# The first MLP product of a hybrid decoder layer, by Strassen's seven block products

## The chip, the cores and the metric

One core of a Trainium2 chip runs the whole layer as one program. The metric is the device time in microseconds; of the kernel before there are three runs, 825.94, 825.32 and 824.52 us, with the median 825.32.

## The reference, cut to what matters

One layer for 512 tokens of 1024 features, in float32. A token mixer of three gated branches (pooling, short convolution, dilated attention) is followed by an MLP with a hidden width of 4096. The change concerns the last two lines:

```python
h = rms_norm(x, norm_mix);  z = h @ w_in            # 1024 -> 7424 columns
merged = g0*(y_pool @ w_pool_up) + g1*(y_conv @ w_conv_out) + g2*(y_attn @ w_attn_up)
x = x + merged @ w_o
h2 = rms_norm(x, norm_mlp)
x = x + square(relu(h2 @ w_ff1)) @ w_ff2            # 1024 -> 4096 -> 1024
```

## The kernel before

Everything is held transposed: features lie on the 128 partitions, the 512 tokens along the free dimension, so x is eight tiles of 128x512. Weights are a stream of units of 128x1024 float32 in the order of use, loaded by SP's queue into three raw buffers (`unit`, L107). `split` (L115) writes each unit as the sum of two float32r parts: ScalarE copies the high part (L118), VectorE subtracts it from the raw unit for the low part (L119). Activations are split in the same way. `mm3` (L122) then makes a float32 product of three float32r matmuls: high by high, high by low, low by high (L125 to L127).

The program is traced in Python and a scheduler lays out each engine's instruction queue: what is ready by its own reckoning goes first, the earlier traced first among these; each queue then runs in that order on the chip, waiting for semaphores.

After the mixer, W_o goes to eight PSUM banks. `x2_evac` (L555) adds a bank to the residual (`res`, L556) and splits it times the norm's gain to `h2` (L164, L167). The first MLP product takes two units at a time, each 128 hidden features by all eight chunks of h2 (L581 to L587): 32 units, 24 matmuls of 128x512 each. 1/rms of x comes later, from squares on ScalarE (L196), their sum over the eight tiles on GpSimd (L200) and over partitions by a matmul with ones (L204); as it is positive, it is multiplied in after the product (L576), with the relu, and ScalarE squares (L577). The second product accumulates eight banks over 32 units (L602 to L610), and the residual is added and stored (L613, L614). All tiles of the mixer keep their memory to the end; the 32 hidden tiles take over those of `br` and `mg`.

Of the kernel before, what the change touches and what calls it, by code (L numbers as in the profile page):

```python
# [11 lines left out]
F32 = mybir.dt.float32  # L12
# [6 lines left out]
P = 128  # L19
# [16 lines left out]
NFF = 32  # L36
AHEAD = 1  # units of weights split ahead of their use
WARM = 9  # products of zeros that wake the tensor engine's clock until the first data is there
# [11 lines left out]
def z_order():  # L50
    """The 128-column chunks of w_in, as (kind, index, first column), in the order of use."""
    def qkv(p):
        return [(n, (g, p), off + (2 * g + p) * P)
                for g in range(3) for n, off in (("q", OFF_Q), ("k", OFF_K), ("v", OFF_V))]

    def conv(i):
        return [(n, i, off + i * P) for n, off in (("cc", OFF_C), ("cx", OFF_X), ("cb", OFF_B))]

    pool = [("pool", g, OFF_POOL + g * P) for g in range(4)]
    z = qkv(0) + conv(0) + conv(1) + qkv(1) + pool + conv(2) + conv(3)  # L60
    gates = [[("gate", (n, m), OFF_G + n * D + m * P) for n in range(3)] for m in range(KC)]
    return z, gates
# [3 lines left out]
def hybrid_layer(ctx: ExitStack, tc: tile.TileContext, xT, wst, pmix, vecs, consts, outT):  # L66
# [4 lines left out]
    wpool = ctx.enter_context(tc.tile_pool(name="wpool", bufs=3))  # L71
    apool = ctx.enter_context(tc.tile_pool(name="apool", bufs=1))
    ps = ctx.enter_context(tc.tile_pool(name="ps", bufs=8, space=PSUM))
# [10 lines left out]
    def tmp(dt=F32):  # L84
        return apool.tile([P, S], dt, tag="tmp", bufs=13, name=nm("tmp"))

# [11 lines left out]

# [1 line left out]
    ahead = deque()  # L100
    rp = None
    n_loaded = [0]

    def raw_unit():
        return wpool.tile([P, 1024], F32, tag="raw", bufs=3, name=nm("raw"))

    def unit():  # L107
        while len(ahead) <= AHEAD and n_loaded[0] < wst.shape[0]:
            raw = raw_unit()
            nc.sync.dma_start(raw, wst[n_loaded[0]])  # L110
            ahead.append(split(raw, rp if n_loaded[0] in LONG else wpool))
            n_loaded[0] += 1
        return ahead.popleft()
# [17 lines left out]

# [1 line left out]
    warm = cpool.tile([P, S], BF16, name="warm")  # L133
    nc.vector.memset(warm, 0.0)
# [16 lines left out]
    n_loaded[0] = KC // 2  # L151
    cst = cpool.tile([P, NCONST], F32, name="cst")
    nc.sync.dma_start(cst, consts)
# [4 lines left out]
    nc.vector.memset(epst, EPS)  # L158
    bd = cpool.tile([P, P], F32R, name="bd")

# [9 lines left out]
    def rsqrt_start(total, n):  # L170
        """1 / sqrt(total / n + EPS): by ln and exp, and what then takes one Newton step in float32."""
        v = tmp()
        nc.scalar.activation(v, total, AF.Identity, scale=1.0 / n, bias=epst)
        y = tmp()
        nc.scalar.activation(y, v, AF.Ln)
        nc.scalar.activation(y, y, AF.Exp, scale=-0.5)
        t = tmp()
        nc.scalar.activation(t, y, AF.Square)

        def newton(out):  # L180
            nc.vector.scalar_tensor_tensor(t, t, -0.5, v, op0=OP.mult, op1=OP.mult)
            out = t if out is None else out
            nc.vector.scalar_tensor_tensor(out, t, 1.5, y, op0=OP.add, op1=OP.mult)
            return out

        return newton

    class Rstd:
        """1 / rms over the features, from their squares as they come in."""

# [11 lines left out]
        def end(self, name):  # L202
            b = bank()
            nc.tensor.matmul(b, ones, self.acc, start=True, stop=True)  # L204
            r = cpool.tile([P, S], F32, name=name)
# [27 lines left out]

    # Work that hangs on a chunk of z goes on in steps, one after each later chunk.
    side = deque()
# [9 lines left out]

# [1 line left out]
    at = ExitStack()  # L247
    atp = at.enter_context(tc.tile_pool(name="atp", bufs=1))
# [34 lines left out]
    def v_evac(kind, idx, b):  # L283
# [20 lines left out]
    def attention(p):  # L304
        """Heads 2p and 2p + 1 of each group; keys on partitions. The groups' mixture is one softmax
        over the keys of all three: one maximum, one denominator."""
        q = [qkv["q", (g, p)] for g in range(3)]
# [65 lines left out]
        for h in range(2):  # L373
# [34 lines left out]

# [1 line left out]
    cu = [atp.tile([P, S + 2], F32, name=f"cu{i}") for i in range(2)]  # L410
# [29 lines left out]
    def load_mix():  # L440
        raw = raw_unit()
        nc.sync.dma_start(raw[:, :4 * P], pmix)
        hi = cpool.tile([P, 4 * P], F32R, name="mixh")
        lo = cpool.tile([P, 4 * P], F32R, name="mixl")
        nc.scalar.activation(hi, raw[:, :4 * P], AF.Copy)
# [51 lines left out]

# [1 line left out]
    res = []  # L499
# [12 lines left out]
    for m in range(KC):  # L512
# [10 lines left out]
        if m == 0:  # L523
            while side:
                pump()
            at.close()
            rp = ctx.enter_context(tc.tile_pool(name="rp", bufs=1))
            for k in range(KC):
                t = rp.tile([P, S], F32, name=f"res{k}")
# [17 lines left out]
        if m >= 1:  # L547
# [3 lines left out]
            wo_mm(0, m - 1, wo_banks[:4])  # L551
    h2 = [None] * KC
    rs2 = Rstd()

    def x2_evac(m):  # L555
        nc.vector.tensor_tensor(res[m], res[m], wo_banks[m], OP.add)  # L556
        h2[m] = split_gain(res[m], vec[:, V_NF + m:V_NF + m + 1], True)

    for i in range(4, 8):
# [3 lines left out]
    wo_mm(0, KC - 1, wo_banks[:4])  # L563
    for m in range(4):
        x2_evac(m)
    wo_mm(1, KC - 1, wo_banks[4:])
    for m in range(4, 8):
        x2_evac(m)

# [1 line left out]
    f = []  # L571

    def ff1_evac(pair):
        for b in pair:
            t = br(F32) if len(f) < 20 else mg(F32)
            nc.vector.scalar_tensor_tensor(t, b, 0.0, rstd2, op0=OP.max, op1=OP.mult)  # L576
            nc.scalar.activation(t, t, AF.Square)  # L577
            f.append(t)

    done = []  # L580
    for j in range(0, NFF, 2):  # L581
        pair = [bank(), bank()]
        w2 = [unit(), unit()]
        for ks in ([range(4)] + [range(k, k + 1) for k in range(4, KC)] if j == 0 else [range(KC)]):
            for b, w in zip(pair, w2):
                for k in ks:
                    mm3(b, w, cols(k), h2[k], k == 0, k == KC - 1)  # L587
        done.append(pair)
        if j == 0:
            for t in res:  # L590
                rs2.add(t)
        if j >= 2:
            if j == 2:
                rstd2 = rs2.end("rstd2")
            for pair in done:
                ff1_evac(pair)
            done = []

# [9 lines left out]
    for m in range(KC):  # L608
# [3 lines left out]
        for t, eng in zip(parts, (nc.sync, nc.scalar)):  # L612
            nc.vector.tensor_tensor(res[m][:, t], res[m][:, t], outs[m][:, t], OP.add)  # L613
            eng.dma_start(outT[:, m, t], res[m][:, t])  # L614


def _chunk(w, c):
    """Columns c..c+127 of w: [1024, n] as a unit [128, 8 * 128]."""
    return w[:, c:c + P].reshape(KC, P, P).transpose(1, 0, 2).reshape(P, KC * P)


def _stream(w_in, w_pool_up, w_conv_out, w_attn_up, w_o, w_ff1, w_ff2):
# [23 lines left out]
    for kk in range(4):  # L646
        units.append(wo(1, kk))
    for j in range(NFF):
        units.append(_chunk(w_ff1, j * P))
    for k in range(NFF):  # L650
# [54 lines left out]
```

## Time and profile before

| | |
|---|---|
| median of three runs | 825.32 us |
| profiled execution, first to last instruction | 822.6 us |
| TensorE matmul / weight load busy | 807.4 / 662.4 us |
| VectorE, ScalarE, GpSimd busy | 424.2, 297.7, 63.2 us |
| first MLP product | 464.95 to 644.42 us |
| second MLP product | from 644.42 us, last matmul about 818.7 us |

Of the profiled execution the page gives the span alone; the median of the timed runs stands 2.7 us above it. In the profile PE is TensorE's matmul, PEld its weight load, DVE VectorE, ACT ScalarE, POOL GpSimd, SP the engine that issues most DMAs. A busy time is the sum of an engine's instruction records; matmul records overlap one another, so the spacing of their starts, not their length, tells their rate.

### The profile page before, as it was taken

What the parts mean: (1) busy time and instruction counts of PE and PEld (TensorE: products, weight loads), DVE (VectorE), ACT (ScalarE), POOL (GpSimd) and SP (SyncE); (2) the same over time, 40 slices, a digit from 0 to 9 for tenths busy, and PEclk for the clock granted to TensorE, in tenths of its full rate; (3) what the DMA queues carried; (4) which work ended last, traced back from release to release, by engine and by line L of the source; (5) the groups of instructions that cost most, each with busy time, mean ns of one, the idle gap of its engine ahead of it and who ended that gap; (6) DMA issues with size and microseconds to landing.
All of it is one profiled execution on the core that took longest, in us unless ns stands there. A gap on an engine that the chain in (4) does not pass through costs nothing. (4 is left out here: it accounts for less than half of the span.)

```text
span 822.6 us, 9086 instructions
## 1 busy us (share of the span) xinstructions
PE 807.4 (98%) x3649; PEld 662.4 (81%) x3649; DVE 424.2 (52%) x530; ACT 297.7 (36%) x398; POOL 63.2 (8%) x50
## 2 busy tenths in 40 slices
PE   7999998999999999999999999999999999999998
PEld 4888787887888888888888778888888888888886
DVE  7659686786885434554343756333333333333323
ACT  5466255742363223322232527233223332233210
POOL 6020012124200000000000320000000000000000
PEclk9999999999999999999999999999999999999999
DMA  6422221221254222222222222222222232222312
GB/s 226 154 78 82 97 77 52 90 103 52 77 166 142 100 79 103 103 102 89 91 102 77 73 106 103 96 85 102 103 103 88 91 103 102 99 83 101 102 52 102
DMA packets 24810, 80.99 MB, mean 98 GB/s; under 512 B 2880, under 2 KB 3136, under 8 KB 24768
## 3 DMA queue, kind: packets, MB, share of 16 engines
q1 hardware_dynamic: 23472, 78.19, 27.3%
q10 hardware_dynamic: 1296, 2.23, 0.9%
q8 instruction: 28, 0.46, 0.2%
q14 instruction: 14, 0.11, 0.0%
HBM read 78.31 MB, written 2.10 MB: 98 GB/s over the span
## 5 line engine op out<-in xcount | busy, mean ns | idle before, releaser
L118 ACT ACTIVATE wh<-raw 128x1024 fp32r<-128x1024 f32 x136 | 144.0, 1060 | 406.6 <-issue 212.4
L127 PE MATMUL bank<-xs,wl 128*128 128x512 f32 x720 | 280.7, 390 | 3.6 <-DVE wl L220 2.4
L125 PE MATMUL bank<-xs,wh 128*128 128x512 f32 x720 | 282.0, 393 | 1.8 <-ACT tmp L196 1.8
L126 PE MATMUL bank<-xs,wh 128*128 128x512 f32 x720 | 280.9, 390 | 2.3 <-DVE xs L167 2.2
L119 DVE TENSOR_TENSOR wl<-raw,wh 128x1024 fp32r<-128x1024 f32 x136 | 170.1, 1252 | 68.5 <-ACT wh L118 64.0
L127 PEld LDWEIGHTS bank<-xs,wl 128*128 128x128 f32 x720 | 135.2, 188 | 33.2 <-DVE wl L220 3.4
L126 PEld LDWEIGHTS bank<-xs,wh 128*128 128x128 f32 x720 | 135.2, 188 | 32.9 <-DVE xs L167 4.8
L125 PEld LDWEIGHTS bank<-xs,wh 128*128 128x128 f32 x720 | 135.1, 188 | 31.8 <-ACT tmp L196 2.7
L126 PE MATMUL bank<-tmp,wh 128*128 128x512 f32 x256 | 99.6, 389 | 0.0
L125 PE MATMUL bank<-tmp,wh 128*128 128x512 f32 x256 | 99.6, 389 | 0.0
L127 PE MATMUL bank<-tmp,wl 128*128 128x512 f32 x256 | 99.6, 390 | 0.0
L127 PEld LDWEIGHTS bank<-tmp,wl 128*128 128x128 f32 x256 | 48.0, 188 | 10.2 <-DVE wl L119 0.3
L126 PEld LDWEIGHTS bank<-tmp,wh 128*128 128x128 f32 x256 | 48.1, 188 | 10.0
L125 PEld LDWEIGHTS bank<-tmp,wh 128*128 128x128 f32 x256 | 48.1, 188 | 9.9
L518 DVE TENSOR_TENSOR tmp<-bank,rstd 128x512 f32<-128x512 f32 x24 | 16.6, 692 | 65.5 <-PE bank L127 65.4
L200 POOL TENSOR_TENSOR tmp<-tmp,tmp 128x512 f32<-128x512 f32 x14 | 23.6, 1688 | 247.7 <-ACT tmp L196 246.8
L406 DVE TENSOR_TENSOR tmp<-br,tmp 128x512 fp32r<-128x512 f32 x20 | 13.6, 690 | 44.4 <-PE bank L126 44.4
L576 DVE SCALAR_TENSOR_TENSOR br<-bank,rstd 128x512 f32<-128x512 f32 x20 | 13.5, 689 | 42.9 <-PE bank L127 42.8
L125 PE MATMUL bank<-br,wh 128*128 128x512 f32 x80 | 31.1, 389 | 0.0
L127 PE MATMUL bank<-br,wl 128*128 128x512 f32 x80 | 31.1, 389 | 0.0
L126 PE MATMUL bank<-br,wh 128*128 128x512 f32 x80 | 31.1, 389 | 0.0
L543 DVE TENSOR_TENSOR tmp<-tmp,bank 128x512 f32<-128x512 f32 x24 | 16.5, 688 | 26.0 <-PE bank L127 26.0
(129 smaller groups left out, 671.1 us busy)
## 6 DMA issues: line engine op xcount, KB each, us to landing
raw<-wst SPq DMA_DIRECT2D x136, 512.0 KB, 3.2
raw<-wst SPq DMA_DIRECT2D x8, 256.0 KB, 5.0
mg<-xT SPq DMA_DIRECT2D x8, 256.0 KB, 5.1
res<-xT ACTq DMA_DIRECT2D x8, 256.0 KB, 4.7
outT<-res SPq DMA_DIRECT2D x7, 256.0 KB, 2.0
cst<-consts SPq DMA_DIRECT2D x1, 416.0 KB, 5.4
raw<-pmix SPq DMA_DIRECT2D x1, 256.0 KB, 2.5
outT<-res SPq DMA_DIRECT2D x1, 128.0 KB, 1.8
```

The lines of the kernel that those rows point to most:

```text
L118: nc.scalar.activation(hi, raw, AF.Copy)
L119: nc.vector.tensor_tensor(lo, raw, hi.bitcast(F32), OP.subtract)
L125: nc.tensor.matmul(out, wh[:, cols], xh, start=start, stop=False)
L126: nc.tensor.matmul(out, wh[:, cols], xl, start=False, stop=False)
L127: nc.tensor.matmul(out, wl[:, cols], xh, start=False, stop=stop)
L200: nc.gpsimd.tensor_tensor(self.acc, self.acc, sq, OP.add)
L406: nc.vector.tensor_tensor(lo, t, hi.bitcast(F32), OP.subtract)
L518: nc.vector.tensor_tensor(t, b, rstd, OP.mult)
L543: nc.vector.tensor_tensor(t, t, b, OP.mult)
L576: nc.vector.scalar_tensor_tensor(t, b, 0.0, rstd2, op0=OP.max, op1=OP.mult)
```

## The change

The first MLP product is cut in eight groups of four units. A group is the product of a 2x2 arrangement of weight blocks (512 input features by 256 hidden features each, b11, b12, b21, b22) with a 2x2 arrangement of activation blocks (512 features by 256 tokens, a11, a12, a21, a22; the second index is that of the features, the first that of the tokens). Strassen's scheme, in Winograd's form, makes it from seven block products where there were eight. The weight sums u, t2, t3, t4 are made for each group by GpSimd from the raw units before the split; so seven forms are split where there were four units. The activation sums s1 to s4 are made and split once, in the first group. Each block product is 24 matmuls of 128x256 (H = 256), and up to three forms are split ahead (FORMS_AHEAD = 2, three buffers). Products add up in three banks A, R, T; ScalarE copies two of them (x1, x5), and VectorE adds and subtracts the rest together. Q4 of a group is traced after Q5 of the next. The mixer's buffers are closed after W_o (`front.close()`), and the MLP's pools are laid over that memory, each new tile waiting for the old tiles under it. The residual sums are all traced together, and h2 is no longer split directly: ScalarE writes `hs`, from which the forms are made. The stream orders w_ff1 by blocks. The rest moves tiles between pools of the same sizes, and comments go.

```diff
 def unit():
-    while len(ahead) <= AHEAD and n_loaded[0] < wst.shape[0]:
+    while len(ahead) <= AHEAD and n_loaded[0] < end[0]:
...
+    front.close()
+    fpool = right(back, "fpool", reuse_waits="tile")
+    spool = right(sm, "spool", reuse_waits="tile")
+    tmps[:] = [fpool, 6]
...
+    def split_form(name, t):
+        hi, lo = form_tile(name + "h", F32R), form_tile(name + "l", F32R)
+        nc.scalar.activation(hi, t, AF.Copy)
+        nc.vector.tensor_tensor(lo, t, hi.bitcast(F32), OP.subtract)
+        return hi, lo
...
+    def tw():
+        return fpool.tile([P, 1024], F32, tag="tw", bufs=5, name=nm("tw"))
+    def w_sum(a, b, out=None):
+        out = tw() if out is None else out
+        nc.gpsimd.tensor_tensor(out, a, b, OP.add)
+        return out
...
+    def w1_forms():
+        t4 = None
+        for g in range(NFF // 4):
+            b11 = w_raw()
+            yield "P1", b11
+            b12 = tw()
+            nc.sync.dma_start(b12, wst[n_loaded[0]])
+            n_loaded[0] += 1
+            u = w_sum(b11, b12)
+            yield "Q5", u
+            if g:
+                yield "Q4", t4
+            b22 = w_raw()
+            t2 = w_sum(u, b22)
+            yield "Q6", t2
+            b21 = w_raw()
+            yield "P2", b21
+            yield "Q3", b22
+            t3 = w_sum(b12, b22)
+            yield "Q7", t3
+            t4 = w_sum(t2, b21, t2)
+        yield "Q4", t4
...
+    def w_form(kind):
+        while len(ready) <= FORMS_AHEAD:
...
+            ready.append((nxt[0], split(nxt[1], wpool)))
...
+    for m in range(KC):
+        nc.vector.tensor_tensor(res[m], res[m], wo_banks[m], OP.add)
+        nc.scalar.activation(hs[m // 4][:, m % 4], res[m], AF.Copy, scale=vec[:, V_NF + m:V_NF + m + 1])
...
+    def product(kind, out, start, stop):
+        (wh, wl), (xh, xl) = w_form(kind), sx[kind]
+        for b in range(2):
+            for k in range(4):
+                w = cols(4 * b + k)
+                first, last = start and b == 0 and k == 0, stop and b == 1 and k == 3
+                o = out[:, b * H:(b + 1) * H]
+                nc.tensor.matmul(o, wh[:, w], xh[:, k], start=first, stop=False, skip_group_check=True)
+                nc.tensor.matmul(o, wh[:, w], xl[:, k], start=False, stop=False, skip_group_check=True)
+                nc.tensor.matmul(o, wl[:, w], xh[:, k], start=False, stop=last, skip_group_check=True)
...
+    sx["P1"] = split_form("a11", a11)
+    for g in range(NFF // 4):
+        A, R, T = bank(), bank(), bank()
...
+        product("P1", A, True, True)
+        x1 = tmp()
+        nc.scalar.activation(x1, A, AF.Copy)
+        if g == 0:
+            s1 = s_diff("s1", a21, a22)
+            sx["Q5"] = split_form("s1", s1)
+            s2 = s_diff("s2", a11, s1)
+            sx["Q6"] = split_form("s2", s2)
+        product("Q5", T, True, True)
+        x5 = tmp()
+        nc.scalar.activation(x5, T, AF.Copy)
+        if late:
+            late()
+        if g == 0:
+            sx["P2"] = split_form("a12", a12)
+            sx["Q3"] = split_form("s4", s_diff("s4", a12, s2))
+            sx["Q7"] = split_form("s3", s_diff("s3", a21, a11))
...
+            nc.scalar.activation(n22, a22, AF.Copy, scale=-1.0)
+            sx["Q4"] = split_form("a22", n22)
+        product("Q6", R, True, True)
+        v1 = tmp()
+        nc.vector.tensor_tensor(v1, R, x1, OP.subtract)
+        if g == 0:
+            for t in res:
+                rs2.add(t)
+            rstd2 = rs2.end("rstd2")
+        ft = ftile("f")
+        product("P2", A, False, True)
+        relu_sq(ft[:, 0:2, :H], halves(A), 0)
+        product("Q3", T, False, True)
+        nc.vector.tensor_tensor(ft[:, 2:4, :H], halves(v1), halves(T), OP.add)
+        product("Q7", R, False, True)
+        v2 = tmp()
+        nc.vector.tensor_tensor(v2, R, x1, OP.subtract)
+        nc.vector.tensor_tensor(ft[:, 2:4, H:], halves(v2), halves(x5), OP.add)
...
+        nc.vector.scalar_tensor_tensor(ft[:, 2:4], ft[:, 2:4], 0.0, r2, op0=OP.max, op1=OP.mult)
+        nc.scalar.activation(ft[:, 2:4], ft[:, 2:4], AF.Square)
...
+        def late(R=R, x1=x1, ft=ft):
+            product("Q4", R, False, True)
+            c = ft[:, 0:2, H:]
+            nc.vector.tensor_tensor(c, halves(x1), halves(R), OP.subtract)
+            relu_sq(c, c, 1)
+            nc.scalar.activation(ft[:, 0:2], ft[:, 0:2], AF.Square)
...
+    late()
+    end[0] = wst.shape[0]
+    sm.close()
+    opool = right(back, "opool", reuse_waits="tile")
```

## Rows read from the trace of the kernel before

**Rows 1.** the page's part 1: engine, busy us (share of span), instructions

```profile
PE 807.4 (98%) x3649; PEld 662.4 (81%) x3649; DVE 424.2 (52%) x530; ACT 297.7 (36%) x398; POOL 63.2 (8%) x50
```

**Rows 2.** the page's part 4, the chain: shares by engine, then by line

```profile
PE 42%; DVE 0%; DVEq 0%; issue 0%
PE bank L127 14%; PE bank L126 14%; PE bank L125 14%; DVE xs L167 0%; PE bank L204 0%; DVE res L613 0%; DVEq L700 0%
```

**Rows 3.** busy us by stretch, engines with (x records), clock, DMA share, GB/s

```profile
464.95:480.00 15.05, 12.07 (x48) 8.40 (x47) 13.71 (x12) 7.26 (x13) 12.08 (x7) 1.00 0.19 71
491.20:644.42 153.22, 153.22 (x675) 126.58 (x674) 60.11 (x67) 54.91 (x72) 0.00 (x0) 1.00 0.28 97
644.42:818.70 174.28, 174.28 (x769) 143.97 (x767) 60.25 (x64) 45.39 (x56) 0.00 (x0) 1.00 0.26 92
```

**Rows 4.** the page's part 5, one weight-load group: busy us, mean ns, idle

```profile
L126 PEld LDWEIGHTS bank<-xs,wh 128*128 128x128 f32 x720 | 135.2, 188 | 32.9 <-DVE xs L167 4.8
```

**Rows 5.** timeline in the first product: start us, us, engine, line, operation

```profile
519.98 0.39 PE L125 MATMUL bank<-xs,wh 128*128 128x512 f32 x1
519.98 0.19 PEld L126 LDWEIGHTS bank<-xs,wh 128*128 128x128 f32 x1
520.21 0.39 PE L126 MATMUL bank<-xs,wh 128*128 128x512 f32 x1
```

**Rows 6.** timeline of TensorE in attention

```profile
119.74 0.39 PE L379 MATMUL bank<-br,vx 128*128 128x128 f32 x2
119.97 0.39 PE L380 MATMUL bank<-br,vx 128*128 128x128 f32 x2
120.19 0.39 PE L379 MATMUL bank<-br,vx 128*128 128x128 f32 x2
```

**Rows 7.** VectorE's groups from 500 to 640 us, busy us and mean ns

```profile
L119 DVE TENSOR_TENSOR wl<-raw,wh 128x1024 fp32r<-128x1024 f32 x26 | 31.9, 1225 | 5.5 <-ACT wh L118 5.5
L576 DVE SCALAR_TENSOR_TENSOR br<-bank,rstd 128x512 f32<-128x512 f32 x19 | 12.8, 689 | 42.9 <-PE bank L127 42.8
```

**Rows 8.** GpSimd's sums by line: ns min/median/max, first and last start

```profile
L456 POOL TENSOR_TENSOR pu<-pu x10: 1039/1040/1887, 173.1 to 199.6; 128x512 f32<-128x512 f32 x10
...
L269 POOL TENSOR_TENSOR tmp<-tmp,tmp x12: 1264/1297/2201, 38.8 to 164.7; 128x512 fp32r<-128x512 f32 x12
```

**Rows 9.** timelines of GpSimd and VectorE where both work

```profile
173.08 1.04 POOL L456 TENSOR_TENSOR pu<-pu 128x512 f32<-128x512 f32 x1 [6.15 <-DVE pu L452]
...
173.14 2.06 DVE L119 TENSOR_TENSOR wl<-raw,wh 128x1024 fp32r<-128x1024 f32 x1
...
464.54 12.97 POOL L200 TENSOR_TENSOR tmp<-tmp,tmp 128x512 f32<-128x512 f32 x7 [239.79 <-ACT tmp L196]
...
464.88 0.68 DVE L556 TENSOR_TENSOR res<-res,bank 128x512 f32<-128x512 f32 x1
...
468.45 2.31 DVE L119 TENSOR_TENSOR wl<-raw,wh 128x1024 fp32r<-128x1024 f32 x1
```

**Rows 10.** timeline of VectorE, first and last operation around the first product

```profile
460.39 0.69 DVE L556 TENSOR_TENSOR res<-res,bank 128x512 f32<-128x512 f32 x1 [1.31 <-PE bank L127]
...
644.62 0.69 DVE L576 SCALAR_TENSOR_TENSOR mg<-bank,rstd 128x512 f32<-128x512 f32 x1 [3.30 <-PE bank L127]
```

**Rows 11.** ScalarE's groups: a weight's high part, a bank read

```profile
L118 ACT ACTIVATE wh<-raw 128x1024 fp32r<-128x1024 f32 x136 | 144.0, 1060 | 406.6 <-issue 212.4
...
L173 ACT ACTIVATE tmp<-bank,epst 128x512 f32<-128x512 f32 x14 | 9.4, 674 | 2.8 <-PE bank L204 2.7
```

**Rows 12.** the page's part 6: DMA issues, count, size, us to landing

```profile
raw<-wst SPq DMA_DIRECT2D x136, 512.0 KB, 3.2
```

**Rows 13.** busy us of one stretch in attention, clock before the DMA share

```profile
130.00:140.00 10.00, 8.60 (x45) 7.86 (x46) 8.93 (x11) 6.91 (x10) 2.96 (x2) 0.83 0.15 54
```

More of the change, by code (lines that the diff above doesn't have):

```diff
@@ L37 @@
 AHEAD = 1
+FORMS_AHEAD = 2
 WARM = 9
@@ L100, in hybrid_layer @@
     ahead = deque()
-    rp = None
+    lp = None
     n_loaded = [0]
+    end = [wst.shape[0] - 2 * NFF]
     def raw_unit():
@@ L107, in unit @@
     def unit():
-        while len(ahead) <= AHEAD and n_loaded[0] < wst.shape[0]:
+        while len(ahead) <= AHEAD and n_loaded[0] < end[0]:
             raw = raw_unit()
             nc.sync.dma_start(raw, wst[n_loaded[0]])
-            ahead.append(split(raw, rp if n_loaded[0] in LONG else wpool))
+            ahead.append(split(raw, lp if n_loaded[0] in LONG else wpool))
             n_loaded[0] += 1
@@ L204, in end @@
             nc.tensor.matmul(b, ones, self.acc, start=True, stop=True)
-            r = cpool.tile([P, S], F32, name=name)
+            r = (zpool if name == "rstd" else cpool).tile([P, S], F32, name=name)
             return rsqrt_start(b, D)(r)
@@ L563, in hybrid_layer @@
     wo_mm(0, KC - 1, wo_banks[:4])
-    for m in range(4):
-        x2_evac(m)
     wo_mm(1, KC - 1, wo_banks[4:])
-    for m in range(4, 8):
-        x2_evac(m)
-    f = []
[L573 to L589, printed above, removed]
+    front.close()
@@ new lines, in w_raw @@
+    def w_raw():
+        raw = raw_unit()
+        nc.sync.dma_start(raw, wst[n_loaded[0]])
+        n_loaded[0] += 1
+        return raw
+    def tw():
[11 more added lines that the diff above has]
+            nc.sync.dma_start(b12, wst[n_loaded[0]])
+            n_loaded[0] += 1
+            u = w_sum(b11, b12)
[12 more added lines that the diff above has]
+        yield "Q4", t4
@@ new lines, in hybrid_layer @@
+    forms = w1_forms()
+    ready = deque()
+    def w_form(kind):
+        while len(ready) <= FORMS_AHEAD:
+            nxt = next(forms, None)
+            if nxt is None:
+                break
+            ready.append((nxt[0], split(nxt[1], wpool)))
+        k, w = ready.popleft()
+        assert k == kind
+        return w
+    rs2 = Rstd()
+    hs = [ftile("hs") for _ in range(2)]
+    for m in range(KC):
+        nc.vector.tensor_tensor(res[m], res[m], wo_banks[m], OP.add)
+        nc.scalar.activation(hs[m // 4][:, m % 4], res[m], AF.Copy, scale=vec[:, V_NF + m:V_NF + m + 1])
@@ new lines, in hybrid_layer, with s_diff @@
+    a11, a21 = hs[0][:, :, :H], hs[0][:, :, H:]
+    a12, a22 = hs[1][:, :, :H], hs[1][:, :, H:]
+    sx = {}
+    def s_diff(name, a, b):
+        t = ftile(name)[:, 0:2].rearrange("p a (b c) -> p (a b) c", c=H)
+        nc.vector.tensor_tensor(t, a, b, OP.subtract)
+        return t
+    def product(kind, out, start, stop):
[8 more added lines that the diff above has]
+                nc.tensor.matmul(o, wl[:, w], xh[:, k], start=False, stop=last, skip_group_check=True)
@@ new lines, in hybrid_layer, with halves, relu_sq @@
+    f = []
+    late = None
+    def halves(ap):
+        return ap.rearrange("p (b t) -> p b t", b=2)
+    def relu_sq(out, c, h):
+        r = rstd2[:, h * H:(h + 1) * H].unsqueeze(1).to_broadcast([P, 2, H])
+        nc.vector.scalar_tensor_tensor(out, c, 0.0, r, op0=OP.max, op1=OP.mult)
+    sx["P1"] = split_form("a11", a11)
+    for g in range(NFF // 4):
+        A, R, T = bank(), bank(), bank()
+        ft = None
+        product("P1", A, True, True)
[15 more added lines that the diff above has]
+            sx["Q7"] = split_form("s3", s_diff("s3", a21, a11))
+            n22 = ftile("n22")[:, 0:2].rearrange("p a (b c) -> p (a b) c", c=H)
+            nc.scalar.activation(n22, a22, AF.Copy, scale=-1.0)
[4 more added lines that the diff above has]
+        if g == 0:
@@ L590, in hybrid_layer @@
             for t in res:
                 rs2.add(t)
[L592 to L597, printed above, removed]
+            rstd2 = rs2.end("rstd2")
[5 more added lines that the diff above has]
+        product("Q7", R, False, True)
@@ L599, in hybrid_layer @@
+        f += [ft[:, i] for i in range(4)]
+    late()
+    end[0] = wst.shape[0]
+    sm.close()
+    opool = right(back, "opool", reuse_waits="tile")
+    tmps[:] = [opool, 10]
     outs = [bank() for _ in range(8)]
@@ L647, in _stream @@
         units.append(wo(1, kk))
-    for j in range(NFF):
-        units.append(_chunk(w_ff1, j * P))
+    for g in range(NFF // 4):
+        blocks = w_ff1[:, 512 * g:512 * g + 512].reshape(2, 4, P, 2, 2, P)
+        for kh, ch in ((0, 0), (0, 1), (1, 1), (1, 0)):
+            units.append(blocks[kh, :, :, ch].transpose(1, 2, 0, 3).reshape(P, 1024))
     for k in range(NFF):
```

36 lines of the change are left out of this document (23 added, 13 removed).

## The prediction

> **What bounds the kernel now.** I read the page's busy table first, then the chain of waits, then a table by stretches, then single instructions. TensorE is busy 98% of the span and nobody else is over 52% [rows 1]; the chain that ended last is the three matmul lines of `mm3`, and nothing else takes more than 0.2% of it [rows 2]. So the kernel is a stream of matmuls. The table by stretches shows what the change can touch [rows 3]: the first MLP product runs from 464.95 to 644.42 us, 179.5 us, at the full granted clock, and the second product behind it takes 174.28 us for 769 records, 226.6 ns a matmul of 512 columns (768 are in the program). The first product is the same 768 matmuls, 174.0 us, and about 5 us of waits, nearly all in its first 15 us. There VectorE is busy 13.71 of 15.05 us, TensorE only 12.07, and GpSimd 12.08. In the long middle, 491 to 644 us, VectorE has 60.11 of 153.22 us and GpSimd nothing. That slack is what the change spends.
>
> **TensorE.** 32 chunks x 8 x 3 = 768 matmuls of 512 columns become 8 groups x 7 products x 24 = 1344 of 256 columns. No row shows a float32r matmul of 256 columns. Lower end: half of 226.6, 113.3 ns, so 152.3 us. [...] I take 116 ns, between the two ends: 155.9 us, 19.5 us a group, against 174.0 / 8 = 21.75 us before. [...]
>
> [...]
>
> **VectorE, each group of four units.** Before: four weight splits and four evacuations. After: seven splits of 128x1024 at 1.225 us, 8.58 us; five 128x512 operations that read a PSUM bank (v1, the relu of A, the sum with T, v2, the difference with R) at 0.69, 3.45 us; two of that size with both inputs in SBUF (v2 + x5, the last relu), 1.38; one 128x1024 relu with both in SBUF, priced as a split, 1.23 [rows 7]. Sum 14.64 us of the 19.5, so alone it would hide.
>
> **GpSimd, each group.** Four sums of 128x1024. [...] Ends: 1.04 (no growth with size) and 2 x 1.30 = 2.6 (the sums that write float32r).
>
> The price that decides is that these two engines stop each other. A split that starts 0.06 us after a pooling sum takes 2.06 us instead of 1.23, about what is left of the sum's 1.04; a split among the squares' sums takes 2.31, while seven of those sums take 12.97 us, 1.85 each; and an operation that reads PSUM keeps its 0.68 in the same stretch [rows 9]. So a VectorE operation with two SBUF inputs and a GpSimd sum take turns. Of VectorE's 14.64 us, 11.19 are such operations, 0.76. I take that share of each sum as lost to VectorE: 8.3 x 0.76 = 6.3, so 21.0 us a group, over TensorE's 19.5: **VectorE becomes the bound**, at hardly less than the 21.75 of before. Ends: nothing lost, 14.64 (TensorE binds); all lost, 23.0.
>
> [...]
>
> **The first group.** It makes the seven activation forms besides. On VectorE these are four differences (s1, s2, s4, s3) and seven low parts, eleven operations of 128x1024, 13.5 us, with the eight residual sums (0.68 each, 5.5 us) and the last two steps of 1/rms (1.4 us). Before, that start already filled VectorE [rows 3]. TensorE can do little meanwhile: P1 needs a11 split, Q5 needs s1 split, Q6 needs s2 of s1, and each is a difference, a ScalarE copy and a subtraction away.
>
> **The sum, along VectorE's queue**, from the first residual sum at 460.39 [rows 10]: 5.5 + 13.5 + 1.4 + 8 x 14.64 = 137.5 us of its own; turns lost to GpSimd, (32 x 2.08 + 7 x 1.04) x 0.76 = 56 us, where the seven are the sums of squares as before; and 3 us, an estimate, in which the queue itself stands still (such waits for TensorE and ScalarE as the 5 us of the old start). Together 196.5, so to 656.9. Before, VectorE's last operation of this product started at 644.62 and took 0.69 [rows 10], to 645.3. That is +11.6 us. The second product is untouched, 174.3 us, and the tail too. The profiled execution lasts 822.6 us in its span; the median of the runs shown is 825.32, 2.7 above it, and I carry that: 822.6 + 11.6 + 2.7 = **837 us**.
>
> **Edits that I cost at nothing, and their cover.** ScalarE: seven high parts at 1.06, two bank copies at 0.67 and two squares of 1024 priced as copies, about 10.9 us of 21 a group [rows 11]; if its cover goes, it is late by one operation, 1 us, in each group. DMA: the same 32 units of 512 KB, 3.2 us from issue to landing [rows 12], two by the raw buffers and SP's queue as before; b12 goes to its own buffer in the same queue. Holding it there ties the queue to GpSimd: the next load in that buffer waits for the sum that frees it, and the loads behind wait too, but five such buffers are more than a group's worth, so I take nothing; if that cover is gone, one load, 3.2 us, in a group. The overlay: the new buffers lie where the mixer's were and wait for their last readers, at the latest the last W_o matmul, so hs could start at 464.95 instead of 460.39: between 0 and 4.6 us; I take 0, since most of the mixer's tiles are done long before. New waits: x1 and x5 are copied by ScalarE, and v1, v2 and the relus of VectorE wait for products; behind them in VectorE's queue stand the low parts of the weights for two products on, for which TensorE then waits; that is in the 3 us. The granted clock: after a gap in attention it was 0.83 over 10 us [rows 13]; a like dip in the first group would cost 0 to 5 us, taken as 0 as TensorE waits there anyway.
>
> **Rivals.**
> A, *TensorE stays the bound* (faster). For it: GpSimd's sums hang on no product, so they can run while VectorE reads PSUM or stands idle, 3.45 + 4.9 us a group, just the 8.3 they need. Against it: a queue in order seldom falls so well, and in the old start VectorE's splits met the sums every time [rows 9]. It decides if fewer than about 0.58 of each sum is lost (14.64 + 8.3 x 0.58 = 19.5). Then seven groups at 19.5, 136.5, behind a first group of about 31 (13.5 + 1.4 + 14.64 on VectorE, and 1.5 lost) and a start of 5 us, the rest of W_o: 460.4 + 172.5 = 632.9, 11.5 us before 644.42: 814 us.
> B, *the sums are dearer*, 2.6 us: lost turns (83.2 + 7 x 1.3) x 0.76 = 70, 14 us over my 56: 851 us. For it: every add on GpSimd outside pooling took 1.26 us or more [rows 8]. Against: those write float32r or were waiting their turn.
> C, *the weight load doesn't hide behind 256 columns*: 1344 x 188 = 252.7 us, 78.7 over the 174.0: 904 us. For it the 188 ns record [rows 4]; against it the 112 ns pace [rows 6]. [...]
>
> **How the numbers follow.** Mine 0.55 (829 to 848 for its own part: a lost share of 0.65 to 0.9), A 0.26, B 0.10, C 0.04, and 0.05 for a draw between mine and A. From no change this kernel can tell 0.2%, 1.7 us. Faster is A, 0.26; same 0.05; slower is mine, B and C, 0.69. A with matmuls of 113.3 ns ends seven groups of 0.46 us earlier, at 811. The range goes from there to B's 851; outside lie C, the dearer half of B and about a third of A, 0.18.
>
> **What would show it.** Right: between 500 and 640 us VectorE is busy over nine tenths, low parts of the weights have a mean well over 1.225 (near 1.8), GpSimd's sums one near or over 2.1, and TensorE waits in every group, mostly for a `wl`; first matmul to first matmul of neighbouring groups is 21 us. The first group takes over 28 us. Wrong: TensorE without gaps from the second group on (A); sums of 2.6 us without VectorE beside them (B); matmuls of 256 columns spaced at 188 ns (C); or a stage that ends before 644 us.

## The result and the profile after

The changed kernel takes 849.27 us (median of 4 runs, 848.67 to 851.99) against 825.63 us of the kernel before beside it: ratio 1.0294, 95% interval 1.0273 to 1.0315. It is slower by 23.6 us, where 11.6 were forecast; the profiled spans differ by 24.3 (846.9 and 822.6).

The busy table of the page of the changed kernel answers to [rows 1]:

```profile
PE 808.6 (95%) x4225; PEld 684.9 (81%) x4225; DVE 518.8 (61%) x589; ACT 336.5 (40%) x430; POOL 159.3 (19%) x82
```

TensorE is busy as long as before, though in the first product 768 matmuls of 226.6 ns have become 1344 of 117.7, 16 us less; VectorE has 95 us more. Where the time lies is in the table by stretches (columns as in [rows 3]): the whole first product along VectorE's queue, ten microseconds in its first group, four steady groups, the first matmuls of the second product, and its long middle.

```profile
463.49:663.31 199.82, 173.86 (x1367) 167.70 (x1365) 177.09 (x143) 104.20 (x119) 105.84 (x39) 0.95 0.26 88
500.00:510.00 10.00, 1.72 (x3) 0.84 (x3) 2.94 (x2) 2.21 (x3) 9.69 (x6) 0.58 0.20 65
553.61:637.59 83.98, 81.15 (x675) 79.52 (x673) 78.60 (x60) 40.26 (x44) 51.16 (x18) 1.00 0.29 101
665.30:669.00 3.70, 3.70 (x9) 2.92 (x10) 3.08 (x5) 2.02 (x4) 0.00 (x0) 0.54 0.43 142
672.00:842.00 170.00, 170.00 (x743) 139.27 (x742) 56.59 (x63) 44.85 (x56) 0.00 (x0) 1.00 0.27 90
```

Read it from below. In the second product, which the change doesn't touch, a matmul takes 170.00 / 743 = 228.8 ns, where [rows 3] gave 226.6, with TensorE never idle and the clock at 1.00. At its start the clock is 0.54. The four groups, from P1, a group's first block product, to the next P1, take 83.98 us, 20.99 each, with VectorE 94% busy. From 500 to 510 us TensorE has 1.72 us of work, VectorE 2.94, and GpSimd 9.69. What TensorE waited for in the whole span (operation, releaser, us in total, times, longest):

```profile
PE bank L214 <- POOL tmp L210: 9.0, 1, 9.0
PE bank L674 <- DVE wl L129: 6.4, 9, 1.7
PE bank L135 <- ACT tmp L415: 3.4, 1, 3.4
PE bank L673 <- DVE a11l L596: 2.8, 1, 2.8
PE bank L672 <- ACT a11h L595: 2.5, 1, 2.5
PE bank L673 <- DVE s4l L596: 2.2, 1, 2.2
```

The longest wait is not for a weight: L214 is the ones matmul that sums the squares for 1 / rms. The timeline of all engines around it (start us, us, engine, line, operation):

```profile
496.49 3.30 POOL L611 TENSOR_TENSOR tw<-tw,raw 128x1024 f32<-128x1024 f32 x1 [1.16 <-DVE wl L129]
...
499.04 0.28 PE L674 MATMUL bank<-s3h,wl 128*128 128x256 f32 x1
...
499.76 8.47 POOL L210 TENSOR_TENSOR tmp<-tmp,tmp 128x512 f32<-128x512 f32 x5
...
508.28 2.07 PE L214 MATMUL bank<-tmp,ones 128*128 128x512 f32 x2 [8.96 <-POOL tmp L210]
...
509.37 1.20 PE L672 MATMUL bank<-a11h,wh 128*128 128x256 f32 x1
```

GpSimd's queue held a weight sum between the second and the third sum of squares; five of those then run one after the other, TensorE's next instruction needs the last, and the next group's P1 stands behind it. The squares themselves come late. These are the first of them on ScalarE and the ones matmul in the kernel before, which waits for nothing, and then the first squares and their sums after the change:

```profile
461.75 0.62 ACT L196 ACTIVATE tmp<-res 128x512 f32<-128x512 f32 x1
491.19 1.02 PE L204 MATMUL bank<-tmp,ones 128*128 128x512 f32 x2
```

```profile
490.21 1.66 ACT L206 ACTIVATE tmp<-res 128x512 f32<-128x512 f32 x3
491.42 3.90 POOL L210 TENSOR_TENSOR tmp<-tmp,tmp 128x512 f32<-128x512 f32 x2 [1.68 <-ACT tmp L206]
```

Before, the squares began with the residual sums, and their sums [rows 9] were done 13.7 us ahead of the ones matmul. Now they come behind the forms of the first group.

### The profile page after: what moved, and what is told of

It is laid out like the page before. It is cut to its first block, busy times and chain, and to the rows that moved or that the text cites. A ratio compares the mean times of both kernels' runs of the same rounds, so it can differ in the third digit from the quotient of the medians.

```text
span 846.9 us, 10401 instructions
## 1 busy us (share of the span) xinstructions
PE 808.6 (95%) x4225; PEld 684.9 (81%) x4225; DVE 518.8 (61%) x589; ACT 336.5 (40%) x430; POOL 159.3 (19%) x82
## 3 DMA queue, kind: packets, MB, share of 16 engines
q10 hardware_dynamic: 1296, 2.23, 0.9%
## 5 line engine op out<-in xcount | busy, mean ns | idle before, releaser
L135 PE MATMUL bank<-xs,wh 128*128 128x512 f32 x464 | 184.0, 398 | 1.1 <-ACT tmp L206 1.1
L137 PE MATMUL bank<-xs,wl 128*128 128x512 f32 x464 | 181.9, 392 | 2.0 <-DVE wl L230 2.0
L136 PE MATMUL bank<-xs,wh 128*128 128x512 f32 x464 | 182.5, 394 | 0.0
L135 PEld LDWEIGHTS bank<-xs,wh 128*128 128x128 f32 x464 | 87.6, 189 | 22.5 <-ACT tmp L206 2.0
L137 PEld LDWEIGHTS bank<-xs,wl 128*128 128x128 f32 x464 | 87.6, 189 | 22.5 <-DVE wl L230 3.0
L136 PEld LDWEIGHTS bank<-xs,wh 128*128 128x128 f32 x464 | 87.6, 189 | 18.6 <-issue 0.2
L611 POOL TENSOR_TENSOR tw<-tw,raw 128x1024 f32<-128x1024 f32 x24 | 72.6, 3038 | 52.6 <-DMA raw<-wst 31.8
L611 POOL TENSOR_TENSOR tw<-raw,tw 128x1024 f32<-128x1024 f32 x8 | 23.1, 2884 | 260.4 <-DMA tw<-wst 236.4
L129 DVE TENSOR_TENSOR wl<-tw,wh 128x1024 fp32r<-128x1024 f32 x32 | 51.0, 1595 | 6.2 <-ACT wh L128 6.2
L128 ACT ACTIVATE wh<-tw 128x1024 fp32r<-128x1024 f32 x32 | 33.5, 1054 | 32.8 <-PE bank L673 22.3
L279 POOL TENSOR_TENSOR tmp<-tmp,tmp 128x512 fp32r<-128x512 f32 x12 | 18.6, 1547 | 78.2 <-ACT tmp L278 59.1
L136 PE MATMUL bank<-br,wh 128*128 128x512 f32 x80 | 31.4, 393 | 0.0
```

The source lines that it names most:

```text
L128: nc.scalar.activation(hi, raw, AF.Copy)
L129: nc.vector.tensor_tensor(lo, raw, hi.bitcast(F32), OP.subtract)
L279: nc.gpsimd.tensor_tensor(sql, sq, sqh.bitcast(F32), OP.subtract)
L611: nc.gpsimd.tensor_tensor(out, a, b, OP.add)
```

## The experiments

Each run has the kernel before beside it on the same chip. "The change" below is its 849.3 us.

**e1_sides: the kernel before with the change's pools.**

```diff
-    apool = ctx.enter_context(tc.tile_pool(name="apool", bufs=1))
+    zpool = right(front, "zpool")
+    apool = right(front, "apool")
...
-    atp = at.enter_context(tc.tile_pool(name="atp", bufs=1))
+    atp = right(at, "atp")
```

> The kernel before, with only the pools placed as after the change: the mixer's tiles and small constants at the right end of the memory. After the change the 512-column matmuls of the mixer and of the second product go by every 228.8 ns instead of 226.7. Theory P (the place of the operands does it): some 2780 matmuls of 512 columns x 2.1 ns = 5.8 us more, about 831.5 us, the last W_o matmul 3 us later. Rival (it comes with the longer program or the MLP): 825.6 us, 226.7 ns.

831.68 us (831.43 to 833.91), ratio 1.0103 [1.0086, 1.012]: the same instructions, and 7.5 us gone by where the tiles lie, against 5.8 in theory P. The second product's middle in this run:

```profile
655.00:825.00 170.00, 170.00 (x743) 139.31 (x742) 58.33 (x62) 43.80 (x54) 0.00 (x0) 1.00 0.27 90
```

228.8 ns a matmul, the changed kernel's pace.

**e2_nosum: no weight sums** (the forms are split from the plain units; not the layer's product).

```diff
-            u = w_sum(b11, b12)
-            yield "Q5", u
+            yield "Q5", b12
...
-            t4 = w_sum(t2, b21, t2)
-        yield "Q4", t4
+        yield "Q4", b21
```

> The changed kernel with the weight sums left out: each form is split from a raw unit, so the output is not the layer's. Theory T (VectorE and GpSimd take turns, 1.2 us a group over TensorE's 19.8): groups at 19.8 us, 8 us less in seven groups, and the wait for the ones matmul in the first group shrinks from 9 to some 2 us: 830 to 834 us, weight splits at 1.23 us. Rival (VectorE is late by its own work, GpSimd costs it nothing): groups stay at 20.9, 842 us or more.

835.43 us (834.13 to 836.94), ratio 1.014 [1.0125, 1.0155]: 13.8 less than the change, and a little above theory T's 830 to 834. By the starts of P1, the first group takes 31.4 us instead of 38.6 and the next six 20.2 on average instead of 21.4; from the third group on it is 19.8, TensorE's own. The turns with GpSimd are real. The other half of the expectation failed: the wait for the ones matmul didn't shrink to 2 us.

```profile
486.94 13.11 POOL L210 TENSOR_TENSOR tmp<-tmp,tmp 128x512 f32<-128x512 f32 x7 [262.31 <-DVE tmp L708]
...
500.10 2.08 PE L214 MATMUL bank<-tmp,ones 128*128 128x512 f32 x2 [9.20 <-POOL tmp L210]
```

Here GpSimd has nothing but the seven sums of squares, and TensorE still waits 9.2 us. So it takes no weight sum in GpSimd's queue to make the ones matmul late: the squares' sums start four microseconds before TensorE is done with the group (490.9), and take 13.1.

**e3_vsum: the sums on VectorE.**

```diff
-        nc.gpsimd.tensor_tensor(out, a, b, OP.add)
+        nc.vector.tensor_tensor(out, a, b, OP.add)
```

> The changed kernel with the 32 weight sums on VectorE instead of GpSimd. Theory T: VectorE has 14.64 + 4 x 1.225 = 19.5 us of its own a group and no turns to lose, TensorE 19.8: 20.0 to 20.5 us a group instead of 21.0, and the ones matmul is no longer late behind GpSimd's queue: 833 to 841 us, faster than the change though VectorE has more work. Rival (VectorE is late by its own work): 4.9 us more a group, 865 us or more.

840.79 us (839.72 to 844.74), ratio 1.0213 [1.0187, 1.0239]: 8.5 less, though VectorE now does every sum itself. All of it is in the later groups, 19.8 us each from the third on; the first group takes 38.5 as before, and the ones matmul, which was to be no longer late, is waited for 5.5 us. The groups of VectorE show why (busy us, mean ns, idle before), first the changed kernel from 553.61 to 637.59 us, with GpSimd's sums in the same stretch in the fence after it, then this run in the same stretch:

```profile
L129 DVE TENSOR_TENSOR wl<-raw,wh 128x1024 fp32r<-128x1024 f32 x12 | 26.8, 2230 | 3.8 <-ACT wh L128 3.8
L129 DVE TENSOR_TENSOR wl<-tw,wh 128x1024 fp32r<-128x1024 f32 x16 | 26.0, 1623 | 1.3 <-ACT wh L128 1.3
L684 DVE SCALAR_TENSOR_TENSOR f<-f,rstd 128x512 f32<-128x512 f32 x4 | 8.7, 2178 | 0.1
...
L725 DVE TENSOR_TENSOR f<-tmp,tmp 128x512 f32<-128x512 f32 x4 | 4.3, 1064 | 0.1
L684 DVE SCALAR_TENSOR_TENSOR f<-bank,rstd 128x512 f32<-128x512 f32 x4 | 2.7, 684 | 0.0
```

```profile
L611 POOL TENSOR_TENSOR tw<-tw,raw 128x1024 f32<-128x1024 f32 x14 | 44.2, 3176 | 17.3 <-DMA raw<-wst 17.3
```

```profile
L129 DVE TENSOR_TENSOR wl<-tw,wh 128x1024 fp32r<-128x1024 f32 x17 | 20.7, 1220 | 0.7 <-ACT wh L128 0.6
L611 DVE TENSOR_TENSOR tw<-tw,raw 128x1024 f32<-128x1024 f32 x13 | 15.9, 1219 | 0.6 <-DMA raw<-wst 0.4
L129 DVE TENSOR_TENSOR wl<-raw,wh 128x1024 fp32r<-128x1024 f32 x13 | 15.8, 1219 | 0.5 <-ACT wh L128 0.5
```

A low part of a weight goes from 1.22 us to 1.62 or 2.23 beside GpSimd, the relu with both inputs in SBUF from 0.69 to 2.18, and the relu that reads PSUM keeps 0.684. A sum costs VectorE 1.22 us when it does it itself. When GpSimd does it, VectorE loses (2230 - 1219) x 12 + (1623 - 1219) x 16 + (2178 - 690) x 4 + (1064 - 690) x 4 ns = 26.0 us over the four groups' 16 to 18 sums, about 1.5 us each, and GpSimd needs 3.18. In these rows the loss falls on operations with two SBUF inputs, and the one with a PSUM input has none; what makes the two engines take turns, no run shows.

**e4_rlate: 1 / rms out of the first product**, its squares in the third group, the sums of the second product multiplied by 1 / mean square.

```diff
-        nc.vector.scalar_tensor_tensor(out, c, 0.0, r, op0=OP.max, op1=OP.mult)
+        nc.vector.tensor_scalar(out, c, 0.0, None, op0=OP.max)
...
-        if g == 0:
+        if g == 2:
...
-            nc.vector.tensor_tensor(res[m][:, t], res[m][:, t], outs[m][:, t], OP.add)
+            y = tmp()[:, t]
+            nc.vector.tensor_tensor(y, outs[m][:, t], rstd2[:, t], OP.mult)
+            nc.vector.tensor_tensor(res[m][:, t], res[m][:, t], y, OP.add)
```

> The changed kernel with 1/rms out of the first product: the relu takes no second operand, the squares are summed in the third group, and the output of the second product is multiplied by 1/mean square before the residual is added. Theory W (the 9 us in which TensorE waits in the first group for the ones matmul, behind GpSimd, are lost outright): 9 us less from that, some 3 us less from relus that no longer read two operands from SBUF, 0.7 us more at the end: 836 to 840 us. Rival (VectorE's queue bounds the first group and the wait covers it): 844 to 849 us.

839.82 us (838.68 to 842.1), ratio 1.0196 [1.0176, 1.0216]: 9.5 less, theory W. From 500 to 510 us, the stretch that had 1.72 us of matmuls:

```profile
500.00:510.00 10.00, 10.00 (x87) 10.00 (x86) 9.93 (x9) 5.10 (x6) 5.47 (x2) 1.00 0.21 65
```

The first group goes from 38.6 to 22.9 us. The next six go from 128.2 to 137.4, where the group that the squares and their sums now fall into takes 28.8. The way from the last P1 to the second product is 2.9 shorter: 15.7 - 9.2 + 2.9 = 9.4. Most of these 2.9 us are the wait at the start of the second product, 0.9 us instead of 3.4, which the next run takes away too; so the gains of the two runs don't add up in full.

**e5_noopool: the second product's halves in the old buffers.**

```diff
-    opool = right(back, "opool", reuse_waits="tile")
-    tmps[:] = [opool, 10]
```

> The change without the pool that the second product's halves get to themselves (opool): they come from the six buffers that the first product's converted tokens use. Everything else is as in the changed kernel (849.3 us). Theory H (hand-over): opool lies over the memory of the forms, so the splits of f for the second product are put behind the last squares on ScalarE; TensorE waits 3.4 us for them at the start of the second product and then runs at the half clock for some us. Without opool the splits go ahead of the squares: 844.0 to 847.0 us, the 3.4 us wait gone, and the chain of waits ends its first product 3 to 4 us earlier. Rival I: the splits wait for VectorE's last outputs of the first product anyway, or six buffers make TensorE wait inside the second product: 848.5 us or more, with a wait of 3 us or more still standing at the start of the second product.

845.04 us (843.28 to 846.27), ratio 1.0241 [1.022, 1.0263]: 4.2 less, theory H. ScalarE's timeline at the hand-over, the changed kernel first:

```profile
661.77 1.06 ACT L128 ACTIVATE wh<-raw 128x1024 fp32r<-128x1024 f32 x1 [2.89 <-PE bank L673]
662.74 1.04 ACT L728 ACTIVATE f<-f 128x1024 f32<-128x1024 f32 x1
663.68 1.04 ACT L735 ACTIVATE f<-f 128x1024 f32<-128x1024 f32 x1
664.63 2.69 ACT L415 ACTIVATE tmp<-f 128x512 fp32r<-128x512 f32 x5
```

```profile
658.79 0.62 ACT L415 ACTIVATE tmp<-f 128x512 fp32r<-128x512 f32 x1
661.77 1.06 ACT L128 ACTIVATE wh<-raw 128x1024 fp32r<-128x1024 f32 x1 [2.36 <-PE bank L673]
662.73 1.05 ACT L728 ACTIVATE f<-f 128x1024 f32<-128x1024 f32 x1
663.68 0.61 ACT L415 ACTIVATE tmp<-f 128x512 fp32r<-128x512 f32 x1
```

Without a pool over the forms' memory the first split of f is done six microseconds sooner, and the second product starts at 661.68 instead of 665.30, with the clock at 1.00 instead of 0.54.

**e6_round, e7_likebase, e8_likechg: the same instructions at other addresses.** e6 is the kernel before, e7 is e1_sides, e8 is the change, each with unused tiles as padding and rstd2 beside the residual:

```diff
     zpool = right(front, "zpool")
+    zpool.tile([P, 80], F32, name="zpad")
...
+    right(back, "bpad").tile([P, 272], F32, name="bpad")
     fpool = right(back, "fpool", reuse_waits="tile")
```

> The kernel before, same instructions in the same order, with every 2 KB tile and weight tile moved to begin at a multiple of 2048 bytes in its partition (they begin at 1696 past such a multiple before, all alike; rstd2 moves beside the residual to make room). Theory R (the pace of the 512-column matmuls depends on how the beginnings of the moving operand and of the weights stand to each other, and they stand alike before): no change, 823 to 827 us, 226.7 ns a matmul. Rival L (what counts is where a tile begins, and a beginning at a round address saves one piece of each row read): 800 to 818 us, 219 to 224 ns a matmul.

> The kernel before with the changed kernel's pool sides (831.7 us as run), same instructions in the same order, and 320 bytes of padding on the right side, after which moving operands and weights again begin at the same distance past a multiple of 2048 bytes. Theory R (how the two beginnings stand to each other sets the pace): back to the kernel before, 823.5 to 826.5 us, three matmuls of a product in 680 ns. Rival A (the side itself, that is the far addresses of the moving operands, is the cause): 830.5 to 833 us, three matmuls in 687 ns.

> The changed kernel, same instructions in the same order, with padding (320 bytes under the mixer's pools on the right, 1088 bytes under those of the MLP; rstd2 moved beside the residual) so that all moving operands and weights begin at the same distance past a multiple of 2048 bytes. Theory R: the 512-column matmuls of the mixer and of the second product go back to 226.7 ns: 2016 of them by 2.1 to 2.3 ns give 4.2 to 4.7 us, and the 256-column matmuls perhaps a little: 842.5 to 846 us. Rival A (the side is the cause): 848.5 to 850.5 us.

e6 824.77 us, ratio 0.9996 [0.9982, 1.001]; e7 825.04, ratio 1.0 [0.9986, 1.0014]; e8 845.35, ratio 1.0244 [1.0228, 1.0259]. The times are theory R's in all three: 320 bytes of padding give the 7.5 us of e1_sides back, and with 1088 more under the MLP's pools the change gets 3.9 back. In e7 the second product's middle has eight more matmuls in 170 us, 226.4 ns each:

```profile
648.00:818.00 170.00, 170.00 (x751) 140.47 (x750) 58.89 (x62) 45.41 (x56) 0.00 (x0) 1.00 0.27 90
```

In e8 the 256-column matmuls went the other way, from 117.7 to 120.0 ns start to start. And its 3.9 us are not the pace alone: its second product starts behind the same wait of 3.4 us, but with the clock at 1.00, where the change has 0.54:

```profile
664.15:667.85 3.70, 3.70 (x16) 3.09 (x17) 3.08 (x5) 2.04 (x4) 0.00 (x0) 1.00 0.42 142
```

**e9_pace: the matmuls alone** (none of the layer is computed).

```diff
+        hi, lo = m[:, o:o + n], m[:, o + 512:o + 512 + n]
+        for i in range(count):
+            c = slice((i % 8) * P, (i % 8) * P + P)
+            nc.tensor.matmul(b[:, :n], wh[:, c], hi, start=i == 0, stop=False)
+            nc.tensor.matmul(b[:, :n], wh[:, c], lo, start=False, stop=False)
+            nc.tensor.matmul(b[:, :n], wl[:, c], hi, start=False, stop=i == count - 1)
```

> The disputed cost by itself: none of the layer, only stretches of 72 matmuls each, with the kernel's three passes (high weights by high operand, high by low, low by high), for eight distances between the beginning of the moving operand and that of the weights: 0, 16, 32, 64, 96, 128, 192 and 320 bytes past a multiple of 512, for 512, 256 and 128 columns. No other engine works meanwhile. Theory R (the distance sets the pace; in the kernels a distance of 0 gave 226.7 ns and of 320 and 1088 bytes 228.9 ns at 512 columns, and 120.0 and 117.7 ns at 256): 512 columns 226.7 ns at 0 and 128 bytes, 228.9 at 64, 192 and 320, and 256 columns 120.0 at 0 and 128, 117.7 at 64, 192 and 320. Rival K (the pace comes from what else the kernels read and write at the time, the distance only moves it): all eight distances within 0.5 ns of each other at each width.

Each stretch is 72 matmuls (the records in brackets count those that reach over its ends too). Distances 64 and 128 at 512 columns, 0 and 192 at 256:

```profile
74.72:91.19 16.47, 16.47 (x73) 13.52 (x72) 0.00 (x0) 0.00 (x0) 0.00 (x0) 1.00 0.00 1
108.00:124.80 16.80, 16.80 (x73) 13.51 (x72) 0.00 (x0) 0.00 (x0) 0.00 (x0) 1.00 0.00 1
158.08:166.72 8.64, 8.64 (x74) 8.64 (x72) 0.00 (x0) 0.00 (x0) 0.00 (x0) 1.00 0.01 2
209.32:217.48 8.16, 8.16 (x75) 8.16 (x73) 0.00 (x0) 0.00 (x0) 0.00 (x0) 1.00 0.01 2
```

16.47 / 72 = 228.8 and 16.80 / 72 = 233.3 ns; 8.64 / 72 = 120.0 and 8.16 / 72 = 113.3. Rival K falls: no other engine works, and the pace still differs from stretch to stretch. Theory R holds at 64 and 320 bytes (228.8 and 228.9 ns; 117.8 twice) and at 0 (226.7 and 120.0), but 128 and 192 bytes miss it (233.3 both, instead of 226.7 and 228.9; 118.6 and 113.3 instead of 120.0 and 117.7). So the distance modulo 128 is not the rule, and the runs don't give the rule. Each distance has its own tile and its own PSUM bank in this run, a single one, so it doesn't separate the distance from these two.

**e10_combo, e11_first, e12_tail: what the causes add up to.** e10 has e3, e4, e5 and new addresses; e11 also orders the first group's matmuls by operand, with nine filler matmuls while TensorE waits for a11h, the high part of the form a11; e12 multiplies the outputs in PSUM:

```diff
+                for _ in range(FILL):
+                    nc.tensor.matmul(out, wh[:, :P], wh[:, :S], start=True, stop=True)
...
-            y = tmp()[:, t]
-            nc.vector.tensor_tensor(y, outs[m][:, t], rstd2[:, t], OP.mult)
-            nc.vector.tensor_tensor(res[m][:, t], res[m][:, t], y, OP.add)
+            nc.vector.tensor_tensor(outs[m][:, t], outs[m][:, t], rstd2[:, t], OP.mult)
+            nc.vector.tensor_tensor(res[m][:, t], res[m][:, t], outs[m][:, t], OP.add)
```

> All the edits that the runs pointed to, on the changed kernel: weight sums on VectorE, 1 / rms taken out of the first product and put on the sums of the second, no pool of its own for the second product's halves, and the tiles placed anew (mixer and second product with moving operands a multiple of 1024 bytes from the weights, the forms of the first product at 192 bytes past one, which gave 113.2 ns at 256 columns where the changed kernel has 117.7). Theory S (the causes found are separate): the run without 1 / rms stood at 839.8; about 9 us for the waits on GpSimd's sums, 4.5 to 7 for the 512-column pace, up to 6 for the 256-column pace: 818 to 827 us. Rival O (they are the same microseconds seen from several sides, the first group's waits for the forms remain): 829 us or more, slower than the kernel before.

> The same, and in the first group each product does all its high by high matmuls before those that need the low parts, with nine filler matmuls ahead of its first product, while TensorE waits for the first form anyway (their results are overwritten). Theory C (the first group loses its time to waits for the low parts and to the half clock that follows): 3 to 6 us faster than without, 814 to 823 us, and the granted clock after the last W_o matmul stays near 1. Rival V (VectorE's order sets the first group, not TensorE's): within 1.5 us of the run without.

> The run with the first group reordered (829.5 us), and at the end each output bank is multiplied by 1 / mean square where it stands in PSUM, instead of into one of the six tmp buffers. Theory T (there the first multiplication begins at 814.47 us, when all banks but one are done, since the six buffers hold the last three halves of f until then; VectorE then works off sixteen operations, and ends 8.8 us after the last matmul begins, against 1.2 us in the kernel before): the multiplications follow the banks, the tail shrinks by 6 to 7 us: 821.5 to 824.5 us, a little under the kernel before. Rival U (two operations a bank on VectorE set the tail wherever the product stands): 827 us or more.

e10 832.34 us (830.32 to 833.8), ratio 1.009 [1.0073, 1.0106]: outside theory S and in rival O's range. Its second product starts at 644.48 and its last matmul at 818.49, where the kernel before has 644.42 and 818.49; the 7 us over that kernel are a tail. It comes of e4's and e5's edits together: VectorE ends 1.9 us after the last matmul's start in e4, which still has opool's ten buffers, and 8.8 us in e10 with six. Rival O has a part too, as TensorE still waits 2.5 us for a11h and 2.6 for a11l, the low part, like the change (2.5 and 2.8). e11 829.49 (829.16 to 829.8), ratio 1.0058 [1.0044, 1.0072], 2.9 less, just under theory C's 3 to 6; the clock from 468 to 478 us is 1.00, where e10 has 0.66. Its 814 to 823 us, which built on e10's forecast, are missed. e12 822.82 (819.55 to 825.39), ratio 0.998 [0.9967, 0.9992]: theory T, and 0.2% faster than the kernel before. VectorE at the tail, e11 and then e12:

```profile
814.47 1.29 DVE L774 TENSOR_TENSOR tmp<-bank,rstd 128x512 f32<-128x512 f32 x2 [12.19 <-PE bank L138]
...
823.54 0.42 DVE L774 TENSOR_TENSOR tmp<-bank,rstd 128x256 f32<-128x256 f32 x1
823.99 0.43 DVE L775 TENSOR_TENSOR res<-res,tmp 128x256 f32<-128x256 f32 x1
```

```profile
802.13 1.38 DVE L773 TENSOR_TENSOR bank<-bank,rstd 128x512 f32<-128x512 f32 x2 [0.89 <-PE bank L139]
...
816.44 0.42 DVE L774 TENSOR_TENSOR res<-res,bank 128x256 f32<-128x256 f32 x1
```

With the six tmp buffers held by the last three halves of f, e11's first multiplication starts at 814.47; with none needed, e12's starts at 802.13.

The new place of the forms in e10 shows one thing more. Two of its groups, P1 to P1:

```profile
516.84:535.88 19.04, 19.04 (x170) 19.04 (x169) 18.29 (x19) 11.96 (x15) 5.28 (x3) 1.00 0.27 87
600.97:620.75 19.78, 19.78 (x170) 19.78 (x169) 18.55 (x21) 10.40 (x11) 0.00 (x0) 1.00 0.33 109
```

The first has 19.04 / 168 = 113.3 ns a matmul, the pace that e9 had at 192 bytes, and the second 117.7, with the same tiles in the same places and TensorE never idle.

## Why the prediction was wrong

The direction held, and in the steady groups the mechanism; the size was half of what came. In the profiled spans 24.3 us are to be explained, 11.6 were forecast, and the 12.7 between split at four points of the time axis:

- *Before the product*: VectorE's first residual sum starts at 463.49 instead of 460.39 [rows 10], +3.1. In e8, with the old pace of the 512-column matmuls, it starts at 462.24; e7, the kernel before at that pace, has 464.29 in a profiled run 3.3 us over its median. So this start moves by itself, and how much of the 3.1 is the pace stays open.
- *Along VectorE's queue*: 463.49 to 663.31 is 199.8 us against 196.5 forecast, +3.3.
- *The hand-over*: the second product's first matmul comes at 665.30, 2.0 after the queue's end, where before it came 0.9 ahead of it (644.42 and 645.3), +2.9.
- *The rest*: 665.3 to 846.9 is 181.6 us, before 178.2, +3.4. It is 179.8 in e5, which has the clock at 1.00 from the start, and 178.4 in e8, which has the old pace besides.

So the step that failed most is "**The second product is untouched, 174.3 us, and the tail too**", with what was costed at nothing beside it: 9.4 of the 12.7 lie outside the queue. The overlay's 0 to 4.6 us were looked for in waits of new buffers on old ones. What the new pools cost was the pace of every 512-column matmul (e1, e7 and e8: 7.5 us in the old kernel, 3.9 net in the change), which no wait shows, and a wait nobody had named: opool lies over the forms, so the splits of f stand behind the last squares (e5: 4.2 us, of which 3.4 is the wait and some the clock of 0.54 behind it, though e8 had the wait without the low clock).

The queue's sum came near by luck, as two errors in it nearly cancel. It was 137.5 own + 56 turns + 3 standing still; the trace has 177.1 busy, so 39.6 for turns, and 22.7 idle. The own part was right (without weight sums, in e2, VectorE is busy 136.7 us from 463 to 650). "**3 us, an estimate, in which the queue itself stands still**" is the failed term here: beside TensorE's wait for L214 VectorE stands still for 7.06 of the 10 us from 500 to 510. The prediction had listed new waits behind x1, x5 and the products, and not that the squares would come behind the first group's forms, at 490.21 us instead of 461.75, with the ones matmul right behind that group in TensorE's queue (e4: 9.5 us when they leave the group). The weight sums in GpSimd's queue are not the main reason, as e2 waits 9.2 us without them. Fewer turns were lost than the 56 us: the first sums run beside VectorE's residual sums, which read PSUM and keep 5.49 / 8 = 0.69 us each, and beside a VectorE that stands still they have nothing to take; that this makes up the whole difference is not shown.

Point by point otherwise:
- 256-column matmuls at 116 ns: 117.7. No row shows the 116, an estimate; the runs showed 117.7 in the change, 120.0 in e8 and 113.3 to 120.0 in e9. Their weight loads hide: a load's record lasts 188 ns as before [rows 4], and a matmul and its load go by every 117.7, as in attention every 112, four in 0.45 us [rows 6]. Rival C, at 188, is out.
- The sum on GpSimd at 2.08 us, twice the 1.04 of the pooling sum of half the size [rows 8] and 8.3 a group: no trace shows a sum of 2.08. It took 2.38 where VectorE reads PSUM (4.76 us for two at 464.49) and 3.18 in the steady groups; the 2.38 lies between the forecast and rival B's 2.6. The price that mattered, VectorE's loss, was 6.3 us a group in the forecast and 26.0 / 4 = 6.5 in the trace.
- A steady group 21.0 us: 20.99. VectorE nearly the bound with 94%, low parts near 1.8 us (1.62 and 2.23): right. Rival A needed 19.5; without sums beside it (e2, e3) TensorE does set 19.8.
- The first group over 28 us: 38.6. The ones matmul's 9.0 are its longest wait; without it, in e4, the group takes 22.9.
- The clock: 0 to 5 us, taken as 0. From 500 to 510 it was 0.58; e11, with fewer idle stretches, gained 2.9 in all.

## What to carry to other kernels

Before giving work to GpSimd, count what VectorE operations with two SBUF inputs lose beside it: here a sum cost VectorE 1.5 us on the other engine and 1.22 on its own. When buffers are moved, compare the pace of matmuls that nothing else touches, one long stretch before and after, and look for whatever the new pool lies over in the order of the engines that fill it. When a stage gets a longer start, see that small work which a later stage needs, here the squares, doesn't slip behind it. An algorithm that makes seven block products of eight pays only when its start, its hand-over and its tail are also free: with all of that mended, e12 ends 1.4 us under the kernel before (822.82 and 824.19), of the 18 us (174.0 - 155.9) that TensorE alone had promised. In e12 the first group still takes 25.7 us and the fourth and fifth, right behind the squares, 23.6 and 22.3, where the last ones take TensorE's 19.8.

## What the runs showed of the hardware

The pace of float32r matmuls depends on where their tiles lie: padding alone took a whole kernel from 228.8 to 226.4 ns at 512 columns (e1 and e7), the change from 117.7 to 120.0 at 256 (e8). Alone, in e9, the stretches differ by 3% at 512 columns (226.7 to 233.5 ns) and by 6% at 256 (113.3 to 120.0), with TensorE never idle, the clock at 1.00, and no other engine at work. At 128 columns they gave 110.8 to 111.8 ns. One rule was tried, the distance between the beginnings modulo 128 bytes, and fell. The place isn't all: e10 put its forms 192 bytes past a multiple, where e9 had 113.3 ns, and took 113.3 in its third group but 117.7 in its seventh. So what sets the pace stays open.
